# Swapping the two half-width sum buffers by block, scaling transposed tiles in pairs, and an off-diagonal product in three float32r products

## The chip, the core and the metric

The kernel runs on one core of a Trainium2 chip. Its parts are TensorE (PE in the profile, with its weight loads as PEld), VectorE (DVE), ScalarE (ACT), GpSimd (POOL) and SyncE (SP). SP and POOL issue most transfers. The time is the device time of one launch in microseconds; the kernel before has a median of 1587.96 us over 3 runs (1587.68 to 1588.22).

## The reference

A batch of one, 256 tokens of width 2048, goes through two layers, each with an RMS norm before and a residual after it, and a last RMS norm. Layer 1 is a Mamba-2 mixer with 64 heads of 64 in 8 groups; layer 2 is a forgetting attention with 32 heads of 128.

```python
proj = h @ w_in                                  # z | x,B,C | dt
xbc = silu(causal_depthwise_conv(xbc, conv_w, conv_b))
dt = softplus(dt_raw + dt_bias); a = -exp(a_log)
xdt = xs * dt; acs = cumsum(dt * a)
y = (C B^T * exp(acs_l - acs_s), causal) @ xdt + xs * d_skip
y = gated_group_rmsnorm(y, z, norm_w) @ w_out    # layer 1
q, k, v, z, f = split(h @ w_in)                  # layer 2
logits = q k^T / sqrt(128) + cum_l - cum_s       # cum = cumsum(log_sigmoid(f + b))
y = (softmax(logits, causal) @ v * silu(z)) @ w_out
```

Everything is float32. The reference forms the Mamba mixer in chunks of 64 tokens; the result is that of the one causal sum above.

## The kernel before

**Products.** A large product is made from float32r parts: `act_hi` (ACT) writes the rounded part of an operand, `dve_lo` (DVE) the remainder, and three products, high by high, high by low and low by high, add up in one PSUM bank. Weights come through `prep` (line 153 issues the load on SP) or, for sums of weight blocks, through `prep_sum` (lines 170 to 207). `run` walks a list of parts, each some 2.7 us of PE work or half of that; the weights of a part are loaded, summed and split three parts ahead (`AHEAD`). `later(n, f)` asks for `f` after n parts, and only the PE instructions that it issues are queued behind the part's products.

**Who sets the order.** The program is handed to a planner. It puts every instruction of an engine into one fixed order, by the time at which its inputs and its buffer are planned to be ready, ties by the order of the program. At run time each engine and each queue (SP's and POOL's among them) works strictly through that order.

**Mamba, groups 0 to 7** (`group_units`). A group is made of column tiles: B, C, four tiles of x (two heads each) and 512 columns of z. A tile of x goes through the convolution and SiLU as `xT` (columns on the partitions), then `xa_pe` turns its two blocks of 128 tokens and `xa_dve` scales what stands in PSUM three times: by dt (`xd`), by the decay to the end of the first block (`xg`, first block only), by D (`xa`). `cb_dve` makes `cb`, three 128x128 blocks of C B^T with mask: first by first block of tokens, first by second, second by second. `decay` turns `acsB` (cumulated decays, spread over partitions by a POOL transfer, tag of two buffers) into `ee`; `y_pe` makes the two diagonal blocks (`py`, line 707), `off_pe` the one off the diagonal (`pof`, line 712), one float32 product of 128x128 by 128x512, and `off_dve` scales it by the decay and adds it to `xa`. Then follow `gate`, `norm` (line 755) and the turn for the output product (`out_pe`, `pyt`). Groups 2 to 7 run pair by pair between the parts of the output product of the pair before (`sum_units`).

**Attention, eight rounds of four heads** (`four_heads`). A round has two blocks of 1024 output columns, qk and vz (`block_units`). The first ten k-tiles of a block are multiplied through seven sums of weight blocks, of which three chains are kept, named a, b and c, with two k-tiles per sum; in rounds 1 to 7 a third sum has one k-tile, and is half as wide (512). In the order of a block, `STEPS`, chain a runs from the first step (A0, into `psx`) to the last (A2, into `psy`), chain c is the second step (C0, into `psv`), chain b runs from B0 to B1, the last step but one. The half-width sums of a and b don't lie in the seven `raw` buffers but in `forms`: tags `gh` and `gl` have six buffers each, the forms of x hold five of each through all rounds, and one of each is left. Before the change, a always takes `gh` and b always `gl`:

```python
elif wide < 1024 and name != "c":
    t = gp.tile([P, 7, P], F32, tag="gh" if name == "a" else "gl",
                name=f"sum_{name}").rearrange("p m s -> p (m s)")
```

In the trace, `sum_a<-in_wf_h` and `sum_b<-in_wf_h` on SP are the first loads of the half-width sums; `in_wf_s` belongs to the wide ones. Line 186 issues them. Line 200 adds b to a (step A3), line 193 adds b to `term` (step B1), after which b's buffer is free; a's is free after its last split for A2. Between vz and the next qk of rounds 1 to 5 lies an output product (`out_f`, `psa`, some 22 us); between qk and vz of a round lies nothing.

Of the kernel before, what the change touches and what calls it, by code (L numbers as in the profile page):

```python
# [17 lines left out]
P = 128  # L18
# [51 lines left out]
def hybrid_kernel(ctx: ExitStack, tc: tile.TileContext, a):  # L70
# [33 lines left out]
    def act_hi(out, in_, scale=None):  # L104
        if scale is None:
            nc.scalar.activation(out, in_, AF.Copy)  # L106
        else:
            nc.scalar.activation(out, in_, AF.Copy, scale=scale)  # L108
# [16 lines left out]
    def later(n, fn):  # L125

        events.setdefault(now[0] + 2 * n, []).append(fn)
# [44 lines left out]
    def prep_sum(u):  # L172


        name, src, how = u["chain"]
        wide = u.get("wide", 1024)
        if how == "load":
            if u.get("apart"):
                t = fp[0].tile([P, 1024], F32, tag="sum", name=f"sum_{name}")
            elif wide < 1024 and name != "c":  # L180
                t = gp.tile([P, 7, P], F32, tag="gh" if name == "a" else "gl",
                            name=f"sum_{name}").rearrange("p m s -> p (m s)")
            else:
                t = wp.tile([P, 1024], F32, tag="raw", name=f"sum_{name}", bufs=RAW)
            u["sums"][name] = t[:, :wide]
            nc.sync.dma_start(u["sums"][name], src)
            if wide < 1024 and name == "c":
                u["sums"]["t"] = t = fp[0].tile([P, wide], F32, tag="term", name="term")
                nc.sync.dma_start(t, u["term"])
        elif how == "add" and "term" in u:  # L190
            t = u["sums"]["t"]
            if name == "b":
                nc.vector.tensor_tensor(t, t, u["sums"]["b"], op=ALU.add)
                u["sums"]["b"] = t
            else:
                nc.vector.tensor_tensor(u["sums"][name], u["sums"][name], t, op=ALU.add)
        elif how == "add":
            behind["POOL"] = nc.gpsimd.dma_start(u["sums"][name], src, accum_op=ALU.add).ins  # L198
        else:
            nc.vector.tensor_tensor(u["sums"][name], u["sums"][name], u["sums"][how], op=ALU.add)  # L200
        raw = u["sums"][name]
        wh = wp.tile([P, 1024], F32R, tag="wh", name="wh")[:, :wide]
        wl = wp.tile([P, 1024], F32R, tag="wl", name="wl", bufs=4)[:, :wide]
        act_hi(wh, raw)
        behind["DVE"] = dve_lo(wl, raw, wh).ins
        u["w"][0] = (wh, wl)
        yield
# [379 lines left out]
    def group_units(g):  # L587
# [2 lines left out]
        wait = 5 if g == 0 else 0  # L590
        more = 4 if g == 0 else 0

        def heads_of(tab, i, n):

            ap = tab[:, H0 + 2 * i:H0 + 2 * i + 2].unsqueeze(2).to_broadcast([P, 2, HD])
            return ap.unsqueeze(1).to_broadcast([P, n, 2, HD]) if n > 1 else ap

        def post_b(ps):
            conv_silu(ps, 6 * g, f"BT{g}", lambda o: st.update(B=o))
# [15 lines left out]
        def cb_dve():  # L615
            st["cb"] = cb = lp.tile([P, 384], F32, tag="cb", name=f"cb{g}", bufs=2)
            nc.vector.tensor_tensor(cb, st["pcb"][:, :384], cst[:, C_MQ:C_MQ + 384],
                                    op=ALU.mult)

        def post_x(i):  # L620
            def post(ps):
                conv_silu(ps, 6 * g + 2 + i, f"xT{g}_{i}", lambda o: x_done(i, o))
                later(2 + wait, lambda: load_acs(i))
            return post
# [7 lines left out]
        def x_done(i, o):  # L632
            st[f"x{i}"] = o
            if g == 0:
                later(1 + wait, lambda: xa_pe(i))
                later(2 + wait, lambda: xa_dve(i))
            elif i % 2:
                st["first"], st["then"] = ((cb_pe,), (cb_dve, lambda: st["mul0"]())) if i == 1 else (
                    (lambda: y_pe(0), lambda: y_pe(1)), ())
                later(2, lambda: [f() for f in (lambda: xa_pe(i - 1), lambda: xa_pe(i),  # L640
                                                *st["first"])])
                later(3, lambda: [f() for f in (*st["then"], lambda: xa_dve(i - 1),
                                                lambda: xa_dve(i))])
            later(2 + wait + more, lambda: decay(i))
            if g == 0:
                later(4 + wait + more, lambda: y_pe(i))
            if i == 3:
                if g > 0:
                    later(5, lambda: [y_pe(2), y_pe(3)])
                late = wait + more or 1  # L650
                later(4 + late, off_pe)
                later(5 + late, off_dve)

        def xa_pe(i):
            st[f"pxa{i}"] = pt = bank(psa, "pxa")
            for t in range(T2):
                nc.tensor.transpose(pt[:, t * P:t * P + P], st[f"x{i}"][:, t * P:t * P + P],
                                    ident)

        def xa_dve(i):  # L660
            if i == 0:
                xa = lp.tile([P, 4 * (S + 1)], F32, tag="xa", name=f"xa{g}", bufs=2)
                st["xa"] = xa[:, :T2 * 512].rearrange("p (t c) -> p t c", t=T2)
                xd = lp.tile([P, 4 * (S + 1)], F32, tag="xd", name=f"xd{g}")
                st["xd"] = xd[:, :T2 * 512].rearrange("p (t c) -> p t c", t=T2)
                st["xg"] = lp.tile([P, 512], F32, tag="xg", name=f"xg{g}")
            c = slice(i * P, i * P + P)
            pt = st[f"pxa{i}"]
            pt4 = pt[:, :S].rearrange("p (t h d) -> p t h d", t=T2, h=2)
            d = dts[:, :, H0 + 2 * i:H0 + 2 * i + 2].unsqueeze(3).to_broadcast([P, T2, 2, HD])  # L670
            nc.vector.tensor_tensor(
                st["xd"][:, :, c].rearrange("p t (h d) -> p t h d", h=2), pt4, d, op=ALU.mult)
            nc.vector.tensor_tensor(
                st["xg"][:, c].rearrange("p (h d) -> p h d", h=2), pt4[:, 0],
                heads_of(gdt, i, 1), op=ALU.mult)
            nc.vector.tensor_tensor(
                st["xa"][:, :, c].rearrange("p t (h d) -> p t h d", h=2), pt4,
                heads_of(row[:, R_D:R_D + MH], i, T2), op=ALU.mult)

        def decay(i):  # L680
            ee = lp.tile([P, 2, T2, P], F32, tag="ee", name="ee", bufs=3)
# [17 lines left out]
        def y_pe(i):  # L699
# [3 lines left out]
            for j in range(2):  # L703
                hl = 2 * i + j
                c = slice(hl * HD, hl * HD + HD)
                for t in range(T2):
                    nc.tensor.matmul(st["py"][t][:, c], m[:, j, t, :], st["xd"][:, t, c],  # L707
                                     start=True, stop=True)

        def off_pe():  # L710
            st["pof"] = bank(psa, "pof")
            nc.tensor.matmul(st["pof"], st["cb"][:, P:2 * P], st["xg"], start=True, stop=True)

        def off_dve():
            yo = sp.tile([P, 512], F32, tag="zth", name="yo")
# [291 lines left out]
    def block_units(w_s, w_p, out, scale, done, order):  # L1007
# [71 lines left out]
        for step in order[0]:  # L1079
            if step == "enter":  # L1080
                entering = len(parts)
                continue
            if step in (0, 1):
                parts.append(order[1][step])
                continue
            if step in n_rest:
                n = n_rest[step]
                n_rest[step] += 1
                names = ("v", "y") if step == "L" else ("z", "u")
                u = us[step]  # L1090
                parts.append({"u": u, "h": [n],
                              "mm": lambda u=u, n=n, names=names: mm_rest(u, n, names)})
                if n + 1 == len(u["w"]) and step == "L":
                    parts[-1]["post"] = left if order[0] is not SECOND else (
                        lambda: [left(), later(1, late_form)])
                continue
            chain, term, how, form, name = step
            for p2 in range(len(pairs)):
                u = {"chain": (chain, w_s[p2][term], how), "sums": sums[p2], "w": [None],
                     "wide": 512 * pairs[p2],  # L1100
                     "apart": chain == "b" and p2 == 0 and order[0] is not FIRST}
                if pairs[p2] == 1 and (chain == "c" or term == 1):
                    u["term"] = w_s[p2][1]
                steps[0] += pairs[p2] == 1
                parts.append({"u": u, "h": [0], "long": 1 if pairs[p2] == 2 else steps[0] % 2,
                              "mm": lambda u=u, form=form, name=name, p2=p2:
                                  mm_sum(u, form, name, p2)})
            if (chain, term) in reads:
                parts[-1]["post"] = reads[chain, term]
                if (chain, term) == ("b", 1) and n_rest["R"] == len(us["R"]["w"]):  # L1110
                    parts[-1]["post"] = lambda: [reads["b", 1](), right()]
# [8 lines left out]
    def four_heads(hq, first=()):  # L1120
# [139 lines left out]
        def weights(n):  # L1260
# [3 lines left out]
            if hq == 0:  # L1264
# [1 line left out]
            return [s1[0], s1[1], s2], rest  # L1266

        return [block_units(*weights(n), out, scale, done,
                            (FIRST, first) if hq == n == 0 else (SECOND if hq == 0 else STEPS, ()))
                for n, (out, scale, done) in enumerate((  # L1270
                    (lambda: bp.tile([P, T2, 1024], F32, tag=f"x{hq % 2}", name=f"qk{hq}"),
                     lambda: lay2["rstQ"], qk_done),
# [174 lines left out]
```

## Time and profile before

| | |
|---|---|
| median of 3 runs | 1587.96 us (1587.68 to 1588.22) |
| the profiled execution | 1588.28 us, its span 1586.5 us |
| granted TensorE clock, mean | 0.999 |
| busy: PE, DVE, ACT, POOL | 1570.5, 1374.1, 1078.5, 178.1 us |
| the share of the span in the chain that ended last: PE, issue, DVE, DMA, ACT | 91, 3, 2, 2, 1% |
| `sum_a<-in_wf_h` on that chain | 1.2% |
| Mamba groups, output products between them | about 5 to 640 us |
| attention rounds and their output products | about 640 us to the end |

A row of the timeline gives the start, the duration, engine, line, operation, output and inputs, how many like instructions stand in the row, and in brackets the idle time before it and what ended it. Matmuls overlap: one of 512 columns is shown as some 390 ns long, while the next starts some 227 ns after it. So what PE loses is read from the starts, not from its busy time.

### The profile page before, as it was taken

The numbers are of one execution on the slowest core, as the hardware profiler recorded it, in microseconds if no ns is written. First come the engines' busy times: TensorE is split into PE (matmuls) and PEld (weight loads), VectorE is DVE, ScalarE is ACT, GpSimd is POOL, SyncE is SP. The second block draws the span as 40 slices with busy tenths as digits, with TensorE's granted clock in tenths as the row PEclk, the third lists the DMA queues.
The fourth block names the chain that finished last, engine by engine and source line by source line (L and its number), as shares of the span: only waits on it lengthen the run. The fifth ranks groups of instructions, "written<-read, shape, count | busy, mean of one in ns | idle before, by whom it ended". The sixth has DMA issues, their size and how long they took to land.

```text
span 1586.5 us, 22866 instructions
## 1 busy us (share of the span) xinstructions
PE 1570.5 (99%) x7760; PEld 1318.8 (83%) x7760; DVE 1374.1 (87%) x2087; ACT 1078.5 (68%) x1694; POOL 178.1 (11%) x225
## 2 busy tenths in 40 slices
PE   9999999999999999999999999999999999999997
PEld 7888888888888888878888888888888888888886
DVE  7897989798979898799888898889888888889886
ACT  7677676767676765766776675766676666777764
POOL 0000111011100110011101110110110111011100
PEclk9999999999999999999999999999999999999999
DMA  9665798769886987579888788798886996899852
GB/s 367 192 215 186 189 276 224 257 177 275 222 265 175 270 226 232 186 170 267 247 246 281 192 231 266 223 227 264 215 259 206 252 276 165 245 270 251 249 178 80
DMA packets 106406, 364.54 MB, mean 230 GB/s; under 512 B 12176, under 2 KB 13072, under 8 KB 106160
## 3 DMA queue, kind: packets, MB, share of 16 engines
q1 hardware_dynamic: 79344, 270.03, 48.6%
q0 software_dynamic: 26800, 92.91, 30.5%
q8 instruction: 61, 1.00, 0.3%
q14 instruction: 57, 0.47, 0.1%
q10 hardware_dynamic: 144, 0.13, 0.0%
HBM read 360.83 MB, written 2.20 MB: 229 GB/s over the span
## 4 chain that ended last, share of the span: by engine, by line
PE 91%; issue 3%; DVE 2%; DMA 2%; ACT 1%; POOL 0%; ACTq 0%; POOLq 0%; DVEq 0%
PE psa L132 22%; PE pst L132 15%; PE psx L132 13%; PE psz L132 10%; PE psv L132 8%; PE psu L132 8%; PE psy L132 7%; PE py L707 2%; DMA sum_a<-in_wf_h 1%; DVE wl L112 1%; PE pqk L1166 1%; PE psc L1184 1%; PE ppt L1216 1%; PE psc L1182 0%; PE po L1242 0%
## 5 line engine op out<-in xcount | busy, mean ns | idle before, releaser
L112 DVE TENSOR_TENSOR wl<-raw,wh 128x1024 fp32r<-128x1024 f32 (+2 forms) x343 | 411.9, 1211 | 52.2 <-issue 22.9
L106 ACT ACTIVATE wh<-raw 128x1024 fp32r<-128x1024 f32 (+2 forms) x343 | 356.1, 1051 | 133.6 <-PE psa L132 54.2
L106 ACT ACTIVATE wh<-sum_a 128x1024 fp32r<-128x1024 f32 (+1 forms) x232 | 220.2, 954 | 157.0 <-PE psu L132 35.6
L112 DVE TENSOR_TENSOR wl<-sum_a,wh 128x1024 fp32r<-128x1024 f32 (+1 forms) x232 | 250.5, 1092 | 23.2 <-ACT wh L106 16.1
L132 PE MATMUL pst<-x,wh 128*128 128x512 f32 (+1 forms) x800 | 204.6, 396 | 0.8 <-DVE wh L161 0.8
L132 PEld LDWEIGHTS pst<-x,wh 128*128 128x128 f32 (+1 forms) x800 | 145.8, 189 | 30.3 <-ACT x L108 1.5
L132 PE MATMUL psa<-wh,x 128*128 128x512 f32 x512 | 129.4, 392 | 0.0
L106 ACT ACTIVATE wh<-sum_b 128x1024 fp32r<-128x1024 f32 (+1 forms) x102 | 100.0, 1004 | 28.2 <-PE psa L132 12.0
L112 DVE TENSOR_TENSOR wl<-sum_b,wh 128x1024 fp32r<-128x1024 f32 (+1 forms) x102 | 115.4, 1146 | 3.8 <-ACT wh L106 2.4
L132 PEld LDWEIGHTS pst<-x,wl 128*128 128x128 f32 x768 | 106.5, 191 | 8.8 <-DVE wl L112 0.3
L132 PEld LDWEIGHTS psa<-wh,x 128*128 128x128 f32 x512 | 95.5, 188 | 20.0 <-issue 0.5
L132 PE MATMUL pst<-x,wl 128*128 128x256 f32 x768 | 109.3, 283 | 0.0
L198 POOL DMA_DIRECT2D sum_a<-in_wf_s x64 | 55.3, 865 | 406.5 <-DMA raw<-in_wf_p 119.9
L132 PE MATMUL psz<-wh,x 128*128 128x512 f32 x200 | 78.7, 393 | 0.0
L132 PE MATMUL psv<-wh,x 128*128 128x512 f32 x200 | 78.2, 391 | 0.0
L132 PE MATMUL psu<-wh,x 128*128 128x512 f32 x200 | 78.0, 390 | 0.0
L132 PE MATMUL psy<-wh,x 128*128 128x512 f32 x200 | 78.0, 390 | 0.0
L132 PE MATMUL psx<-wh,ghx 128*128 128x512 f32 x234 | 77.8, 399 | 0.0
L132 PE MATMUL psx<-wl,ghx 128*128 128x512 f32 x234 | 76.3, 393 | 0.0
L132 PE MATMUL psx<-wh,glx 128*128 128x512 f32 x234 | 76.0, 391 | 0.0
L800 DVE TENSOR_TENSOR xs<-psa,xs 128x512 f32<-128x512 f32 (+1 forms) x81 | 51.9, 679 | 22.6 <-PE psa L132 22.2
L132 PE MATMUL psa<-wh,ghf 128*128 128x512 f32 (+1 forms) x260 | 71.1, 392 | 0.0
(359 smaller groups left out, 3365.3 us busy)
## 6 DMA issues: line engine op xcount, KB each, us to landing
raw<-in_wf_p SPq DMA_DIRECT2D x96, 512.0 KB, 4.7
raw<-in_wm_t SPq DMA_DIRECT2D x90, 512.0 KB, 5.1
raw<-in_wm_z SPq DMA_DIRECT2D x64, 512.0 KB, 5.7
sum_a<-in_wf_s POOLq DMA_DIRECT2D x64, 512.0 KB, 8.5
raw<-in_wf_o SPq DMA_DIRECT2D x64, 512.0 KB, 6.4
sum_a<-in_wm_s POOLq DMA_DIRECT2D x36, 512.0 KB, 6.8
sum_a<-in_wf_s SPq DMA_DIRECT2D x32, 512.0 KB, 6.9
sum_c<-in_wf_s SPq DMA_DIRECT2D x32, 512.0 KB, 9.3
```

The lines of the kernel that those rows point to most:

```text
L106: nc.scalar.activation(out, in_, AF.Copy)
L112: return nc.vector.tensor_tensor(out, in_, hi.bitcast(F32), op=ALU.subtract)
L132: behind["PE"] = nc.tensor.matmul(*args, **kw).ins
L198: behind["POOL"] = nc.gpsimd.dma_start(u["sums"][name], src, accum_op=ALU.add).ins
L707: nc.tensor.matmul(st["py"][t][:, c], m[:, j, t, :], st["xd"][:, t, c], start=True, stop=True)
L800: nc.vector.tensor_tensor(c, pss[t][:, a:b], c, op=ALU.add)
L1166: nc.tensor.transpose(pt[:, n * P:n * P + P], st["qk"][:, t, c:c + FD], ident)
L1184: nc.tensor.matmul(ps[:, P:P + S], q[:, :P], k[:, P:], start=j == 0, stop=j == 2)
L1216: nc.tensor.transpose(pt[:, c:c + P], uu[:, c:c + P], ident)
```

## The change

Three edits. The half-width sums of a and b change places in the second block of a round: a takes `gh` in qk and `gl` in vz, b the other one each time (`order` of `block_units` gets a third entry, true for the block qk). In groups 1 to 7, two tiles of x are turned into one PSUM bank, and each of the three scalings runs over both at once; group 0 stays as it was. In all groups the off-diagonal product is made from float32r parts: the middle block of `cb` is split right after it is made (tile `cbo`, one buffer), `xg` is split in a new step `off_split` one part ahead of `off_pe`, into two tiles under the tag `acsB`, and three products take the place of one.

```diff
@@ -178,7 +178,7 @@
             if u.get("apart"):
                 t = fp[0].tile([P, 1024], F32, tag="sum", name=f"sum_{name}")
             elif wide < 1024 and name != "c":
-                t = gp.tile([P, 7, P], F32, tag="gh" if name == "a" else "gl",
+                t = gp.tile([P, 7, P], F32, tag="gh" if (name == "a") == u["even"] else "gl",
                             name=f"sum_{name}").rearrange("p m s -> p (m s)")
             else:
                 t = wp.tile([P, 1024], F32, tag="raw", name=f"sum_{name}", bufs=RAW)
@@ -590,10 +590,11 @@
         wait = 5 if g == 0 else 0
         more = 4 if g == 0 else 0
 
-        def heads_of(tab, i, n):
-
-            ap = tab[:, H0 + 2 * i:H0 + 2 * i + 2].unsqueeze(2).to_broadcast([P, 2, HD])
-            return ap.unsqueeze(1).to_broadcast([P, n, 2, HD]) if n > 1 else ap
+        def heads_of(tab, i, m, n):
+
+            m *= 2
+            ap = tab[:, H0 + 2 * i:H0 + 2 * i + m].unsqueeze(2).to_broadcast([P, m, HD])
+            return ap.unsqueeze(1).to_broadcast([P, n, m, HD]) if n > 1 else ap
 
         def post_b(ps):
             conv_silu(ps, 6 * g, f"BT{g}", lambda o: st.update(B=o))
@@ -616,6 +617,10 @@
             st["cb"] = cb = lp.tile([P, 384], F32, tag="cb", name=f"cb{g}", bufs=2)
             nc.vector.tensor_tensor(cb, st["pcb"][:, :384], cst[:, C_MQ:C_MQ + 384],
                                     op=ALU.mult)
+
+            st["cbo"] = c2 = lp.tile([P, 2, P], F32R, tag="cbo", name="cbo", bufs=1)
+            act_hi(c2[:, 0], cb[:, P:2 * P])
+            dve_lo(c2[:, 1], cb[:, P:2 * P], c2[:, 0])
 
         def post_x(i):
             def post(ps):
@@ -637,10 +642,9 @@
             elif i % 2:
                 st["first"], st["then"] = ((cb_pe,), (cb_dve, lambda: st["mul0"]())) if i == 1 else (
                     (lambda: y_pe(0), lambda: y_pe(1)), ())
-                later(2, lambda: [f() for f in (lambda: xa_pe(i - 1), lambda: xa_pe(i),
+                later(2, lambda: [f() for f in (lambda: xa_pe(i - 1, 2),
                                                 *st["first"])])
-                later(3, lambda: [f() for f in (*st["then"], lambda: xa_dve(i - 1),
-                                                lambda: xa_dve(i))])
+                later(3, lambda: [f() for f in (*st["then"], lambda: xa_dve(i - 1, 2))])
             later(2 + wait + more, lambda: decay(i))
             if g == 0:
                 later(4 + wait + more, lambda: y_pe(i))
@@ -648,34 +652,38 @@
                 if g > 0:
                     later(5, lambda: [y_pe(2), y_pe(3)])
                 late = wait + more or 1
+                later(3 + late, off_split)
                 later(4 + late, off_pe)
                 later(5 + late, off_dve)
 
-        def xa_pe(i):
+        def xa_pe(i, n=1):
+
             st[f"pxa{i}"] = pt = bank(psa, "pxa")
-            for t in range(T2):
-                nc.tensor.transpose(pt[:, t * P:t * P + P], st[f"x{i}"][:, t * P:t * P + P],
-                                    ident)
-
-        def xa_dve(i):
+            for j in range(n):
+                for t in range(T2):
+                    c = (t * n + j) * P
+                    nc.tensor.transpose(pt[:, c:c + P], st[f"x{i + j}"][:, t * P:t * P + P],
+                                        ident)
+
+        def xa_dve(i, n=1):
             if i == 0:
                 xa = lp.tile([P, 4 * (S + 1)], F32, tag="xa", name=f"xa{g}", bufs=2)
                 st["xa"] = xa[:, :T2 * 512].rearrange("p (t c) -> p t c", t=T2)
                 xd = lp.tile([P, 4 * (S + 1)], F32, tag="xd", name=f"xd{g}")
                 st["xd"] = xd[:, :T2 * 512].rearrange("p (t c) -> p t c", t=T2)
                 st["xg"] = lp.tile([P, 512], F32, tag="xg", name=f"xg{g}")
-            c = slice(i * P, i * P + P)
+            c, m = slice(i * P, i * P + n * P), 2 * n
             pt = st[f"pxa{i}"]
-            pt4 = pt[:, :S].rearrange("p (t h d) -> p t h d", t=T2, h=2)
-            d = dts[:, :, H0 + 2 * i:H0 + 2 * i + 2].unsqueeze(3).to_broadcast([P, T2, 2, HD])
+            pt4 = pt[:, :n * S].rearrange("p (t h d) -> p t h d", t=T2, h=m)
+            d = dts[:, :, H0 + 2 * i:H0 + 2 * i + m].unsqueeze(3).to_broadcast([P, T2, m, HD])
             nc.vector.tensor_tensor(
-                st["xd"][:, :, c].rearrange("p t (h d) -> p t h d", h=2), pt4, d, op=ALU.mult)
+                st["xd"][:, :, c].rearrange("p t (h d) -> p t h d", h=m), pt4, d, op=ALU.mult)
             nc.vector.tensor_tensor(
-                st["xg"][:, c].rearrange("p (h d) -> p h d", h=2), pt4[:, 0],
-                heads_of(gdt, i, 1), op=ALU.mult)
+                st["xg"][:, c].rearrange("p (h d) -> p h d", h=m), pt4[:, 0],
+                heads_of(gdt, i, n, 1), op=ALU.mult)
             nc.vector.tensor_tensor(
-                st["xa"][:, :, c].rearrange("p t (h d) -> p t h d", h=2), pt4,
-                heads_of(row[:, R_D:R_D + MH], i, T2), op=ALU.mult)
+                st["xa"][:, :, c].rearrange("p t (h d) -> p t h d", h=m), pt4,
+                heads_of(row[:, R_D:R_D + MH], i, n, T2), op=ALU.mult)
 
         def decay(i):
             ee = lp.tile([P, 2, T2, P], F32, tag="ee", name="ee", bufs=3)
@@ -707,9 +715,17 @@
                     nc.tensor.matmul(st["py"][t][:, c], m[:, j, t, :], st["xd"][:, t, c],
                                      start=True, stop=True)
 
+        def off_split():
+            st["off"] = xs2 = [lp.tile([P, 512], F32R, tag="acsB", name=f"xg{i}", bufs=2)
+                               for i in "hl"]
+            act_hi(xs2[0], st["xg"])
+            dve_lo(xs2[1], st["xg"], xs2[0])
+
         def off_pe():
             st["pof"] = bank(psa, "pof")
-            nc.tensor.matmul(st["pof"], st["cb"][:, P:2 * P], st["xg"], start=True, stop=True)
+            for n, (i, j) in enumerate(((0, 0), (0, 1), (1, 0))):
+                nc.tensor.matmul(st["pof"], st["cbo"][:, i], st["off"][j],
+                                 start=n == 0, stop=n == 2)
 
         def off_dve():
             yo = sp.tile([P, 512], F32, tag="zth", name="yo")
@@ -1097,7 +1113,7 @@
             chain, term, how, form, name = step
             for p2 in range(len(pairs)):
                 u = {"chain": (chain, w_s[p2][term], how), "sums": sums[p2], "w": [None],
-                     "wide": 512 * pairs[p2],
+                     "wide": 512 * pairs[p2], "even": order[2],
                      "apart": chain == "b" and p2 == 0 and order[0] is not FIRST}
                 if pairs[p2] == 1 and (chain == "c" or term == 1):
                     u["term"] = w_s[p2][1]
@@ -1266,7 +1282,7 @@
             return [s1[0], s1[1], s2], rest
 
         return [block_units(*weights(n), out, scale, done,
-                            (FIRST, first) if hq == n == 0 else (SECOND if hq == 0 else STEPS, ()))
+                            (FIRST if hq == n == 0 else SECOND if hq == 0 else STEPS, first, n == 0))
                 for n, (out, scale, done) in enumerate((
                     (lambda: bp.tile([P, T2, 1024], F32, tag=f"x{hq % 2}", name=f"qk{hq}"),
                      lambda: lay2["rstQ"], qk_done),
```

## The prediction

> **What bounds the kernel now.** I read the page, then the windows by stage, then PE's own waits. A measurement of this kernel can tell about 0.2%, 3.2 us, from no change; every difference below is held against that.
>
> ```profile
> span 1586.5 us, 22866 instructions
> ...
> 160.00:640.00 480.00, 480.00 (x2498) 409.82 (x2497) 427.94 (x670) 326.60 (x490) 56.82 (x73) 1.00 0.82 231
> 740.00:1480.00 740.00, 736.83 (x3492) 613.51 (x3491) 647.06 (x890) 505.08 (x778) 95.11 (x112) 1.00 0.85 238
> ...
> PE psv L132 <- DVE wl L112: 3.2, 7, 0.6
> ```
>
> The columns of the windows are the stretch, its length, then busy PE, PEld, DVE, ACT and POOL. PE is busy for all of the 480 us in which Mamba groups 2 to 7 run, and for 736.8 of 740 us in attention. Its clock is full (1.00). So only two things move the end: less PE work, or fewer PE stalls, and attention has one kind of stall: seven times a product of C0 into `psv` waits for its low split on DVE. What DVE or ACT gains elsewhere is worth nothing by itself.
>
> **One of the stalls in detail** (round 2, qk to vz), in the timeline:
>
> ```profile
> 900.03 0.33 SPq L186 DMA_DIRECT2D sum_b<-in_wf_h  x1
> ...
> 918.48 0.33 SPq L186 DMA_DIRECT2D sum_a<-in_wf_h  x1
> ...
> 923.48 0.63 ACT L106 ACTIVATE wh<-sum_a 128x512 fp32r<-128x512 f32 x1 [3.65 <-DMA sum_a<-in_wf_h]
> ...
> 924.15 0.69 DVE L112 TENSOR_TENSOR wl<-sum_a,wh 128x512 fp32r<-128x512 f32 x1 [1.60 <-ACT wh L106]
> ...
> 925.49 2.96 DVE L112 TENSOR_TENSOR wl<-sum_c,wh 128x1024 fp32r<-128x1024 f32 x3
> ...
> 924.53 0.39 PE L132 MATMUL psx<-wh,glx 128*128 128x512 f32 x1
> 924.89 0.50 PE L132 MATMUL psx<-wl,ghx 128*128 128x512 f32 x1
> 925.24 0.62 PE L132 MATMUL psv<-wh,ghx 128*128 128x512 f32 x2
> 925.69 0.61 PE L132 MATMUL psv<-wh,glx 128*128 128x512 f32 x2
> 926.76 0.73 PE L132 MATMUL psv<-wl,ghx 128*128 128x512 f32 x2 [0.46 <-DVE wl L112]
> 927.33 0.49 PE L1216 MATMUL ppt<-cst,dd 128*128 128x128 f32 x3
> ```
>
> The half-width sum a of vz can only be loaded at 918.48, when `gh` is free of the a of qk, and it is there 4.9 us later. ACT stands 3.65 us, DVE 1.60 us, and the splits of sum c, which stand behind on both in-order engines, come late in their turn. What it costs is in the starts: four products between 925.24 and 926.76 would take 0.91 us at 0.227 each (two starts of 925.24 lie 0.45 before 925.69). From 924.53 to 926.76 six starts take 2.23 us in place of 1.36, and the next two 0.57 in place of 0.45: 0.87 + 0.12 = 0.99 us.
>
> The same load stands on the chain of waits in rounds 3, 4 and 6, and in the queue of round 5:
>
> ```profile
> 1030.32 4.90 DMA sum_a<-in_wf_h
> ...
> 1142.17 4.97 DMA sum_a<-in_wf_h
> ...
> 1365.77 4.93 DMA sum_a<-in_wf_h
> ...
> 1254.09 0.33 SPq L186 DMA_DIRECT2D sum_a<-in_wf_h  x1
> ```
>
> So five of the seven waits are of this kind. Round 1 is the control that the profile holds by chance: there the load is early, ACT stands behind PE and not behind the load, and the same products run at their pace (five starts from 813.86 to 815.00, 1.14 us):
>
> ```profile
> 810.63 0.63 ACT L106 ACTIVATE wh<-sum_a 128x512 fp32r<-128x512 f32 x1 [2.43 <-PE psy L132]
> ...
> 813.86 0.39 PE L132 MATMUL psx<-wl,ghx 128*128 128x512 f32 x1
> ...
> 815.00 0.62 PE L132 MATMUL psv<-wl,ghx 128*128 128x512 f32 x2
> ```
>
> The other two waits are the change of round without an output product between (rounds 0 to 1, 6 to 7):
>
> ```profile
> 761.73 0.61 ACT L106 ACTIVATE wh<-sum_a 128x512 fp32r<-128x512 f32 x1
> ...
> 771.09 0.73 PE L132 MATMUL psv<-wl,ghx 128*128 128x512 f32 x2 [0.57 <-DVE wl L112]
> ...
> 1421.04 0.50 PE L132 MATMUL psv<-wl,ghx 128*128 128x512 f32 x1 [0.39 <-DVE wl L112]
> ```
>
> In the first, the half sum was split 9 us ahead; DVE's order is at fault, and the swap does not touch it. I count nothing for either (bound: at most 0.57 + 0.39 plus a slow restart each, 1.4 us in all).
>
> **The swap.** In vz, a now takes `gl`, which is free where b of qk was done with: the trace already shows a load entering that buffer at 900.03, 18.45 us before 918.48. The load lands by about 905, where the split is asked for near 920. SP gains no instruction; two loads trade places, and the one that now stands earlier is as ready there as b's was. Late next is b of vz: it now enters `gh` at about 918.5 in place of 900. It is wanted by the last third of B0, behind C0, one L and two thirds of B0, or 15 + 12 + 12 products after 925.24: near 925.2 + 39 x 0.227 = 934.1, and its split starts three parts, some 5 us, ahead. With the 4.9 us of landing it is there at 923.4, 5 us early. So the five stalls go: 5 x 0.99 = **5.0 us**. Bounds: nothing gained, if sum c's splits are late without a's help; 5.0 + 1.4 = 6.4 if all seven go.
>
> **The off-diagonal product.**
>
> ```profile
> 616.12 1.08 PE L712 MATMUL pof<-xg,cb 128*128 128x512 f32 x2
> 616.63 1.03 PE L132 MATMUL psx<-wh,ghm 128*128 128x512 f32 x2
> 617.50 0.62 PE L132 MATMUL psx<-wh,glm 128*128 128x512 f32 x2
> ```
>
> One float32 product (two records) and two float32r ones take 617.50 - 616.12 = 1.38 us; without the two, 0.93. Three float32r products take 0.68. PE has no idle time to hide it in, so 0.25 x 8 groups = **2.0 us** are gained. Bounds: none, if the change of operand type costs at the end as it does now (0.93 covers such a restart), to 2.0. The Trainium skill (TensorE: Matmul & The Clock Gate, "Wait — 56ns, not 53.3ns?") gives 215.7 ns from start to start at 512 columns; this trace has 227. By the page alone three products would take 0.65, the gain here would be 2.3 us, and the sum below 0.3 us lower.
>
> The splits add per group, on ACT and on DVE, one instruction of 128x512 (0.63 and 0.69, as at 923.48 and 924.15) and one of 128x128, bounded by the same: at most 1.3 and 1.4 us, hidden while PE doesn't wait for them. `off_pe` now waits for ACT and then DVE after `xg`; behind it on PE waits everything. The narrowest group, and a full split on ACT:
>
> ```profile
> L106 ACT ACTIVATE wh<-raw 128x1024 fp32r<-128x1024 f32 (+2 forms) x343 | 356.1, 1051 | 133.6 <-PE psa L132 54.2
> ...
> 196.10 0.28 DVE L673 TENSOR_TENSOR xg<-pxa,gdt 128x128 f32<-128x128 f32 x1
> 196.30 0.42 DVE L676 TENSOR_TENSOR xa<-pxa,row 128x256 f32<-128x256 f32 x1
> 196.63 0.68 DVE L691 TENSOR_TENSOR ee<-ee,cb 128x512 f32<-128x512 f32 x1
> 197.23 1.22 DVE L112 TENSOR_TENSOR wl<-sum_b,wh 128x1024 fp32r<-128x1024 f32 x1
> ...
> 203.00 1.08 PE L712 MATMUL pof<-xg,cb 128*128 128x512 f32 x2
> ```
>
> From 196.38 to 203.00 there are 6.6 us. The pair of splits takes 1.3, and each full split that stands in front takes about 1.05 on ACT and 1.22 on DVE: one before each makes 3.6 us. Value 0; it begins to cost beyond 6.6.
>
> **The tag `acsB`.** Its two buffers now go to the two halves of `xg` before the next group's decays. I take it that a tag's buffers are handed out in the order of the program; the rows for it, of group 1:
>
> ```profile
> 135.59 1.08 PE L712 MATMUL pof<-xg,cb 128*128 128x512 f32 x2
> ...
> 143.13 1.29 DVE L729 SCALAR_TENSOR_TENSOR zs<-zth,psa 128x512 f32<-128x512 f32 x2 [2.41 <-ACT zth L728]
> 144.34 0.68 DVE L716 TENSOR_TENSOR yo<-pof,fdec 128x512 f32<-128x512 f32 x1
> ```
>
> `yo` shares a tag with `zth`, its input is ready by 136.7, DVE idles 2.41 us, and it still comes after the `zth` that the program names first. So POOL's loads for the next group's first two heads move from before `pof` to behind it, here past the 203.7 at which `pof` ends, and the ACT decays with them; on POOL's own queue they move past loads that add up sums, which can only go earlier for it. The next group multiplies by them a whole group later. Value 0; the bound is a PE that waits at `py`: up to one load and one decay per group, and PE has no such wait now (480 of 480 us).
>
> **Pairs of x tiles.** PE's turns are the same. DVE:
>
> ```profile
> L671 DVE TENSOR_TENSOR xd<-pxa,dts x32: 414/417/425, 67.7 to 606.6; 128x256 f32<-128x256 f32 x32
> L673 DVE TENSOR_TENSOR xg<-pxa,gdt x32: 278/284/294, 68.0 to 606.9; 128x128 f32<-128x128 f32 x32
> ...
> L716 DVE TENSOR_TENSOR yo<-pof,fdec x8: 684/692/694, 96.7 to 617.2; 128x512 f32<-128x512 f32 x8
> ```
>
> Two tiles cost 2 x (417 + 284 + 417) = 2236 ns; as one, about 692 + 417 + 692 = 1801. 14 pairs save 6.1 us of DVE, against at most 8 x 1.4 = 11 that the splits add. PE waits for neither: value 0. If that cover were gone, the difference of at most 5 us would be PE's; if PE had waited for DVE here, up to 6 would be won, but the 480 of 480 us exclude that.
>
> **The sum.** 5.0 + 2.0 = 7.0 us. The profiled execution took 1588.28 (span 1586.5 and 1.8 around it), 0.3 above the median of the runs; 1588.28 - 7.0 = 1581.3, against the median **1581.0 us**.
>
> **The rivals.**
> - *The next wait takes over (20%).* Without the load, the splits of c are still late by DVE's own order, as at 771.09. For it: DVE runs three in a row from 925.49 without idling. Against it: it idled 1.60 just before, more than the 0.99 lost, and round 1. If each of the five gives only a quarter, 1.2 + 2.0 = 3.2: 1584.8.
> - *All seven go (8%).* The planner's order around 1421.04 and 771.09 changes too: 1588.0 - 2.0 - 6.4 = 1579.6.
> - *The off product waits, and the kernel is slower (6%).* With four full splits before each half, the pair ends 4 x 1.05 + 0.63 + 4 x 1.22 + 0.69 = 10.4 us after `xg`. Where 6.6 us are to be had PE stands 3.8 us, and if all eight groups are so narrow, 30 us: 1588 - 7 + 30 = 1611. It decides from 6.6 us on, and outweighs the gain from 7.5 us on (0.9 x 8). Against it: the rows above show three shorter instructions and one full split behind `xg`.
> - *The swap doesn't free a earlier (6%)*, if the planner still puts its load where it was, behind a buffer asked for earlier: only the 2.0 are gained, 1586.0.
>
> **How the numbers follow.** The forecast holds 60%, with its own range 1579.5 to 1583.2 (a planner's order that shifts by a product or two in each round). The first rival's half above 1584.8, the last rival and a little of small losses at PE make "within 0.2%" 0.20; slower 0.06; the rest, 0.74, is faster. For 8 in 10 the range reaches from 1579.2 to 1586.0.
>
> **What would show it.** Swap: `sum_a<-in_wf_h` of vz issued some 18 us earlier and off the chain of waits, ACT's waits for it gone, `psv` waiting for `wl` twice, not seven times. Off product: three records some 0.23 apart per group, in 0.68 us, with no PE idle time before the first. Pairs: three rows of 14 per scaling with 692 and 417 ns. It is wrong if PE gets a wait at `pof`, at `py` or `pyt`, if `psz` waits for the split of b, or if `psv` goes on waiting in rounds 2 to 6.

## The result, and the profile after

Over six runs of each, the changed kernel takes 1601.66 us (1597.42 to 1603.24) against 1588.09 (1585.72 to 1589.93): a ratio of 1.0083, interval 1.0069 to 1.0097. Ratios here and below are of runs at the full granted clock (one of the kernel before, 1733.46 us at 0.85, and one of the sixth experiment, 2894.22 us at 0.779, stand outside) and need not be the quotient of the medians. It is slower by 13.6 us, where 7 us of gain were forecast. Its profiled execution took 1603.24 us. The page, and the same two stretches of the windows as before (Mamba groups 2 to 7, attention), read:

```profile
span 1601.5 us, 22853 instructions
```

```profile
160.00:640.00 480.00, 467.41 (x2426) 397.90 (x2425) 415.71 (x626) 318.44 (x489) 56.61 (x73) 0.99 0.81 224
740.00:1480.00 740.00, 739.77 (x3507) 618.18 (x3506) 652.15 (x897) 510.84 (x776) 96.58 (x114) 1.00 0.86 241
```

Attention did what was forecast: PE idles 0.2 us there in place of 3.2. Mamba did not: PE, which had not idled for 480 us, now idles 12.6, and its records in that stretch fall from 2498 to 2426. Two marks of the trace split the difference. The last Mamba group's first `pyt` starts at 641.53 before and at 662.23 after, 20.7 us later; from there to the end it is 945.0 us before and 939.3 after, 5.7 us less. 20.7 - 5.7 = 15.0, the difference of the spans.

PE's waits name who ends the stops (us in all, times, longest):

```profile
PE psx L132 <- DVE xs L849: 10.5, 6, 2.5
PE pyt L778 <- ACT xa L771: 2.1, 2, 1.8
...
PE psv L132 <- DVE wl L112: 0.2, 1, 0.2
```

Of the places in Mamba that the prediction watched (`pof`, `py`, `pyt`) only `pyt` is among them, and the largest wait, an output product that waits until DVE has added up the sum before it (`xs`, line 849), was not on its list. The waits of all engines show what else grew, ahead of DVE; of after, and then of before:

```profile
POOL acsB L633 <- PE pof L727: 66.1, 6, 23.4
...
ACT ee L693 <- DMA acsB<-acs_d: 39.9, 16, 6.1
```

```profile
POOL acsB L628 <- ACT ee L685: 112.1, 28, 16.4
...
ACT ee L685 <- DMA acsB<-acs_d: 13.4, 7, 3.6
```

The first load of `acsB` for a group waits for the `pof` of the group before, as forecast; ACT's wait for those loads has tripled. The timeline of after, where group 2 ends and group 3's decays are due, ties the two ends together (start, length, engine, in brackets the idle time before it and its end):

```profile
205.54 0.48 PE L727 MATMUL pof<-xgh,cbo 128*128 128x512 f32 x1
...
206.55 1.12 POOL L633 DMA_DIRECT2D acsB<-acs_d  x2 [1.96 <-PE pof L727]
207.45 1.06 ACT L106 ACTIVATE wh<-raw 128x1024 fp32r<-128x1024 f32 x1 [3.27 <-PE psz L132]
...
213.57 0.99 ACT L693 ACTIVATE ee<-acsB,beta 128x128 f32<-128x128 f32 x3 [5.06 <-DMA acsB<-acs_d]
...
214.46 1.04 ACT L106 ACTIVATE wh<-sum_b 128x1024 fp32r<-128x1024 f32 x1
...
215.54 1.22 DVE L112 TENSOR_TENSOR wl<-sum_b,wh 128x1024 fp32r<-128x1024 f32 x1 [3.61 <-ACT wh L106]
...
219.56 0.70 PE L132 MATMUL psx<-wh,ghm 128*128 128x512 f32 x2 [0.80 <-DVE xs L849]
...
229.82 0.68 DVE L849 TENSOR_TENSOR xs<-xs,psx 128x512 f32<-128x512 f32 x1
...
230.65 0.85 PE L132 MATMUL psx<-wh,ghm 128*128 128x512 f32 x2 [2.54 <-DVE xs L849]
```

Read from top to bottom it is a suspicion: the loads are issued behind `pof`, land 7 us later, ACT stands 5.06 us at the first of group 3's decays, the split of `sum_b` stands behind it, DVE stands 3.61 us for that split, and the additions behind it keep `psx` from PE. Before, at the same change, the first two loads were out before `pof` (193.88 and 196.52, `pof` at 203.00), and the first split of `sum_b` ran 6.85 us earlier, of which 2.54 is that this stage as a whole came earlier (`pof` at 203.00, not 205.54):

```profile
203.12 1.57 ACT L685 ACTIVATE ee<-acsB,beta 128x128 f32<-128x128 f32 x5 [1.51 <-DMA acsB<-acs_d]
...
207.61 1.04 ACT L106 ACTIVATE wh<-sum_b 128x1024 fp32r<-128x1024 f32 x1
```

The experiments ask whether it is the lent tag that does it, and through which of the two queues, POOL's or ACT's.

### The profile page after: what moved, and what is told of

It reads as the page before. It is cut to its first block, busy times and chain, and to the rows that moved or that the text cites. A ratio compares the mean times of both kernels' runs of the same rounds, so it can differ in the third digit from the quotient of the medians.

```text
span 1601.5 us, 22853 instructions
## 1 busy us (share of the span) xinstructions
PE 1574.5 (98%) x7768; PEld 1324.0 (83%) x7768; DVE 1377.4 (86%) x2061; ACT 1083.2 (68%) x1710; POOL 177.4 (11%) x225
## 4 chain that ended last, share of the span: by engine, by line
PE 86%; DVE 5%; issue 4%; DMA 2%; ACT 2%; POOL 0%; POOLq 0%; ACTq 0%; DVEq 0%
PE psa L132 21%; PE psx L132 13%; PE pst L132 11%; PE psz L132 9%; PE psv L132 8%; PE psu L132 8%; PE psy L132 8%; DMA acsB<-acs_d 2%; DVE wl L112 2%; PE py L715 2%; ACT wh L106 1%; PE pqk L1182 1%; PE psc L1200 1%; PE ppt L1232 1%; ACT ee L693 1%
## 5 line engine op out<-in xcount | busy, mean ns | idle before, releaser
L132 PE MATMUL pst<-x,wh 128*128 128x512 f32 (+1 forms) x800 | 207.9, 401 | 0.7 <-DVE wh L161 0.7
L112 DVE TENSOR_TENSOR wl<-sum_b,wh 128x1024 fp32r<-128x1024 f32 (+1 forms) x102 | 115.1, 1146 | 16.2 <-ACT wh L106 15.1
L106 ACT ACTIVATE wh<-sum_c 128x1024 fp32r<-128x1024 f32 (+1 forms) x58 | 54.5, 952 | 28.9 <-PE psa L132 17.4
L693 ACT ACTIVATE ee<-acsB,beta 128x128 f32<-128x128 f32 x128 | 42.3, 391 | 46.5 <-DMA acsB<-acs_d 39.9
```

Source lines behind the costliest of these rows:

```text
L112: return nc.vector.tensor_tensor(out, in_, hi.bitcast(F32), op=ALU.subtract)
L132: behind["PE"] = nc.tensor.matmul(*args, **kw).ins
L693: nc.scalar.activation(ee[:, j, t, :], st["acs"][i][:, j, t * P:t * P + P], AF.Relu, scale=-1.0, bias=beta[:, t, h:h + 1])
```

## The experiments

My theory was the chain above. Its rivals were that the two added splits, or the wait of PE for them, cost the time; that the paired tiles do; and that it is POOL's standing 66 us behind `pof`, with its sum loads behind that, and not ACT's.

**The whole change, with the halves of `xg` under another tag.** `zth` belongs to the group's own `yo` and gate, which come after `pof` anyway.

```diff
-            st["off"] = xs2 = [lp.tile([P, 512], F32R, tag="acsB", name=f"xg{i}", bufs=2)
+            st["off"] = xs2 = [sp.tile([P, 512], F32R, tag="zth", name=f"xg{i}")
```

> The whole change, but the two halves of xg lie under the tag zth, so that acsB keeps its two buffers for the decays. Nothing is left out. Theory (the lent acsB buffers cost everything: the loads of the next group's decays move behind pof, ACT's queue stands at their first relu, and the splits behind it come late): the Mamba part falls back from 662 us (last pyt) to about 640, the gains of attention (5.7 us) and of the product (2 us) stay, 1580 to 1583. Rival (the four extra splits per group, or the product's own wait for them, cost it): 1595 or more.

It took 1581.04 us (1579.63 to 1581.89), 0.9958 of before (0.9945 to 0.9971). So one tag turns 13.6 us of loss into 6.7 of gain (by the ratios). The waits of all engines, the windows and ACT's timeline at the same place:

```profile
POOL acsB L633 <- ACT ee L693: 126.8, 30, 15.4
...
ACT ee L693 <- DMA acsB<-acs_d: 12.2, 7, 2.7
```

```profile
160.00:640.00 480.00, 480.00 (x2509) 411.55 (x2508) 429.96 (x643) 330.36 (x502) 56.85 (x73) 1.00 0.82 232
```

```profile
202.14 1.28 ACT L693 ACTIVATE ee<-acsB,beta 128x128 f32<-128x128 f32 x4 [1.88 <-DMA acsB<-acs_d]
...
207.51 1.04 ACT L106 ACTIVATE wh<-sum_b 128x1024 fp32r<-128x1024 f32 x1
```

No load waits for `pof`, ACT's wait for them is what it was before the change, the split of `sum_b` is back at 207.51, and PE doesn't idle. All the splits and pairs are still there, so neither they nor PE's wait for them is the cause.

**The swap alone**, on the kernel before:

```diff
-                t = gp.tile([P, 7, P], F32, tag="gh" if name == "a" else "gl",
+                t = gp.tile([P, 7, P], F32, tag="gh" if (name == "a") == u["even"] else "gl",
```

> The kernel before with the swap of gh and gl alone. Theory: attention's 820.9 us from the first pqk to the end become 815.2, as in the changed kernel, and nothing else moves: 1582 to 1583. Rival (attention is faster because it now starts in another phase of the queues, which the Mamba part set): within 2 us of the kernel before.

1583.57 us, 0.9973 of before (0.9962 to 0.9984): 4.3 us faster, a little short of the 1582 to 1583 expected and clear of the rival's 2 us. The queue of loads and PE's line in round 2:

```profile
899.40 0.33 SPq L186 DMA_DIRECT2D sum_a<-in_wf_h  x1
...
917.85 0.33 SPq L186 DMA_DIRECT2D sum_b<-in_wf_h  x1
...
924.12 0.39 PE L132 MATMUL psx<-wl,ghx 128*128 128x512 f32 x1
...
924.80 0.62 PE L132 MATMUL psv<-wh,glx 128*128 128x512 f32 x2
...
925.26 0.62 PE L132 MATMUL psv<-wl,ghx 128*128 128x512 f32 x2
```

```profile
740.00:1480.00 740.00, 740.00 (x3520) 619.31 (x3519) 652.17 (x902) 513.15 (x790) 98.46 (x116) 1.00 0.85 239
```

The two loads have traded places (899.40 and 917.85), the products run at their pace, and PE does not idle at all in 740 us: all seven waits are gone, not the five.

**The three products alone, with the tag as in the change**, x tile by tile, no swap:

```diff
+            st["off"] = xs2 = [lp.tile([P, 512], F32R, tag="acsB", name=f"xg{i}", bufs=2)
...
-            nc.tensor.matmul(st["pof"], st["cb"][:, P:2 * P], st["xg"], start=True, stop=True)
+            for n, (i, j) in enumerate(((0, 0), (0, 1), (1, 0))):
+                nc.tensor.matmul(st["pof"], st["cbo"][:, i], st["off"][j],
+                                 start=n == 0, stop=n == 2)
```

> The kernel before with the off-diagonal product in three float32r products alone, halves of xg under acsB, x's scalings tile by tile. Theory (lent buffers): the Mamba part loses its 20.7 us here too, 1605 to 1611. Rival (the pairs of x tiles make the loss, by xT and cu that come late): 1585 to 1590.

1601.65 us, 1.0081 of before (1.0058 to 1.0104), less than the 1605 to 1611 expected and far from the rival. The loss is here, without pairs and without the swap, by the same waits:

```profile
POOL acsB L632 <- PE pof L724: 64.9, 6, 25.3
...
ACT ee L690 <- DMA acsB<-acs_d: 30.5, 15, 4.5
```

```profile
PE psx L132 <- DVE xs L846: 6.8, 4, 2.5
```

**The whole change, the tag left lent, but the decays put further back on ACT.** Each decay's ACT instructions are ordered behind the newest weight split:

```diff
-                act_hi(wh[:, c], raw[:, c])
+                behind["ACT"] = act_hi(wh[:, c], raw[:, c]).ins
...
-        act_hi(wh, raw)
+        behind["ACT"] = act_hi(wh, raw).ins
...
+            with tc.issue_after(behind["ACT"]):
+                for j in range(2):
...
+                nc.scalar.activation(ee, ee, AF.Exp, scale=-1.0)
```

> The whole change, acsB lent as in it, but decay's relus and exponential on ACT are queued behind the last split of weights that the program names before them. Theory (what costs is that ACT's in-order queue stands at a relu whose transfer is under way, not that the decays are late): the waits of psx for xs go, 1580 to 1588. Rival (the decays themselves are late, or POOL's queue is what holds the sums): PE waits at py or psx as before, 1598 or more.

1581.64 us, 0.9961 of before (0.9947 to 0.9975). This is the run that tells POOL's queue from ACT's:

```profile
POOL acsB L632 <- PE pof L727: 67.2, 6, 24.6
...
ACT ee L693 <- PE py L715: 6.6, 6, 1.1
```

```profile
205.92 1.06 ACT L106 ACTIVATE wh<-sum_b 128x1024 fp32r<-128x1024 f32 x1 [1.23 <-DVE wl L111]
...
247.79 0.39 ACT L693 ACTIVATE ee<-acsB,beta 128x128 f32<-128x128 f32 x1
```

The loads wait for `pof` as long as in the changed kernel (67.2 us against 66.1), and POOL stands as long, yet the time is that of the first experiment. Only ACT's wait for them is gone: the first decay of the next group runs at 247.79, 45 us after its load was issued (202.74). So the late load costs nothing, and POOL's standing costs nothing; ACT standing in front of the splits costs it all.

**The pairs alone**: `xa_pe` and `xa_dve` with two tiles in groups 1 to 7, on the kernel before.

> The kernel before with x's transposes scaled in pairs alone. Theory (DVE time that no product waits for is worth nothing): within 1.5 us of 1588, the Mamba part (last pyt) at 641.5 within 1 us. Rival (the pair, which waits for the later tile's turns, makes xT and cu late and costs 1 to 3 us in groups 2 to 7): 1590 to 1592.

1586.94 us against 1587.11, ratio 0.9998 (0.9989 to 1.0007), the last `pyt` at 640.99: nothing, though DVE's three scalings do shrink as worked out (the rows of `xd` in the changed kernel: 14 pairs and the 4 tiles of group 0):

```profile
L679 DVE TENSOR_TENSOR xd<-pxa,dts x18: 417/682/692, 67.1 to 627.1; 128x512 f32<-128x512 f32 x14, 128x256 f32<-128x256 f32 x4
```

**The three products alone under `zth`**, the third experiment with the tag of the first:

```diff
-            st["off"] = xs2 = [lp.tile([P, 512], F32R, tag="acsB", name=f"xg{i}", bufs=2)
+            st["off"] = xs2 = [sp.tile([P, 512], F32R, tag="zth", name=f"xg{i}")
```

> The kernel before with the three float32r products alone, the halves of xg under zth. Theory: PE does 8 times 0.24 us less and waits for nothing new: 1586 to 1587. Rival (the splits' place on ACT and DVE takes the gain back): 1588 or more.

1587.45 us against 1587.11, ratio 0.9998 (0.9989 to 1.0007), between the two expectations. This and the third experiment differ in the tag alone: 1.0081 against 0.9998, some 13 us. By itself, the off product in three parts gains nothing that can be measured. Why, the timeline shows:

```profile
615.73 0.48 PE L724 MATMUL pof<-xgh,cbo 128*128 128x512 f32 x1
616.04 0.39 PE L724 MATMUL pof<-xgl,cbo 128*128 128x512 f32 x1
616.27 0.39 PE L724 MATMUL pof<-xgh,cbo 128*128 128x512 f32 x1
616.50 0.63 PE L132 MATMUL psx<-wh,ghm 128*128 128x512 f32 x2
```

From the first start to the next product it is 0.77 us, where the prediction had 0.68 and the float32 product 0.93: the first, which follows the float32 `py`, takes 0.31 to the next start, the others 0.23.

**The swap and the three products under `zth`, x tile by tile**: the first experiment without pairs.

> The swap and the three products with the halves under zth, without the pairs. Theory (the parts add up, and the pairs are worth nothing): the same as the run e1_off_zth_tag within 1 us, 1580 to 1582. Rival (the pairs' 6 us of DVE made room for the four splits): 1583 or more.

1581.43 us, 0.9962 of before (0.9950 to 0.9975), as the first experiment (0.9958): the pairs are worth nothing in company either, and the four splits cost nothing without them.

**Both cures at once**: halves under `zth` and decays behind the splits.

> The whole change with the halves under zth, and the decays on ACT queued behind the splits of weights. Both cures of the one illness: if there is only that illness, the second adds nothing, 1580 to 1582. If decays in ACT's order still cost something with the buffers given back, 1578 to 1580.

1580.67 us, 0.9958 of before (0.9946 to 0.9971). Where ACT no longer stands, holding the decays back adds nothing. Every version that has the swap and doesn't let ACT stand beats both kernels (1580.67 to 1583.57 us); of those with the whole change, the first is the shortest edit.

## Why the prediction was wrong

**The step that failed is "The tag `acsB`", with its "Value 0; the bound is a PE that waits at `py`".** Its mechanism was right as far as it went: a tag's buffers are handed out in the order of the program, and the loads went behind `pof`. It then asked who needs the decays, found that nobody does for a whole group, and priced the delay at nothing. That answer was right too: in the fourth experiment the first of them runs 45 us behind its load (247.79 against 202.74), and it costs nothing. What it left out is what stands behind a decay on ACT: the planner's order has it in front of the splits for the output product, ACT takes its instructions in order, and an input that lands only 7 us after the issue at 206.55 holds up work that has no part in it. The Trainium skill (Perfetto Trace Analysis, "Tensor Engine Instruction (MATMUL, LD_WEIGHTS)") says that ACT, DVE and GpSimd are strict FIFO; the 5.06 us of ACT at 213.57, with a split right behind, agree. The prediction asked just this of POOL's queue and of PE's, and not of ACT's.

Its price can be laid out in the trace of after: 12.6 us of PE idle time in groups 2 to 7; 1.5 more than before at the `pyt` of 154.69, just ahead (1.81 against 0.33); and some 1.6 us in each of three stretches in which PE runs at half pace behind a stop (below), 4.8. Each of the ten added stops hides some 0.16 us more, since a product is shown as 0.39 long where the next could start after 0.227: an estimate of 1.6. That is 20.5, against the 20.7 by which Mamba ends later, plus the 1.2 or so that the off product should have saved there. The 1.4 us left over I can't attribute. Nor is it shown why the lent tag costs Mamba more in the whole change (20.7) than in the third experiment, whose mark is at 656.66 (15.1): its trace has fewer stops (8.4 us in groups 2 to 7) and two stretches at half pace.

**The rival on the slower side** had the wrong place: no run's list of PE's waits names `pof`, so the splits of `xg` fit into the 6.6 us, as worked out. (The `pof` that the prediction lets end at 203.7 ends at 204.08 by its own row; nothing hangs on it.)

**The swap** was right in mechanism: loads at 899.40 and 917.85 where 900 and 918.5 were forecast, off the path, stalls of rounds 2 to 6 gone. Its size was about right too. In the changed kernel the four rounds from 880.05 to 1323.62 take 443.57 us against 447.29 before (859.70 to 1306.99), 0.93 each, the forecast's 0.99 nearly. The rest of the 5.7 us is the two waits at changes of round which I counted at nothing (bound 1.4); all but 0.2 us of them vanished, why is not shown, so the rival "all seven go" was the case. It isn't sure to be: in the first experiment one of them came back, larger (PE's waits list `psv` for `wl` once, 1.6 us), and attention gains 4.4, from 944.97 to 940.58. In the trace of the swap alone it gains 6.1 (to 938.83), while its runs gain 4.3 us by the ratio, with 2.5 to 6.0 as the interval: 5.0 can't be told from 6.4 by them.

**The off product** was priced at 0.25 a group; the trace has 0.15 to 0.16, 1.2 us in eight groups, too little to be seen in the sixth experiment. The term that was sized wrong is "0.68": it took three float32r products at their running pace and left out that the first follows `py` and takes 0.31. The bound below it, a cost at the change of type, pointed the right way.

**The pairs** were right at 0. The cover that they were to give the splits wasn't needed: without pairs the splits cost nothing that can be measured (sixth and seventh experiments), so the bound of 5 us was never tried.

That the first experiment lands on the forecast's 1581.0 is partly luck: between the marks the swap gave 4.4 for 5.0, the off product 1.2 for 2.0, and Mamba in that run ends 2.3 us earlier (639.22 against 641.53), of which only 1.2 has a cause in these rows.

## What to carry to other kernels

When a step delays an input, ask of each engine that reads it not only who needs the result, but what stands behind the reading instruction on that engine's queue: a prefetch that is early by a whole group still has to be there when its reader's turn comes. Buffers lent by a prefetch cost its lead; take them from a tag whose next user comes later anyway, or move the reader back. And a wait's releaser in PE's list (`xs` on DVE here) can be two engines away from the cause, so follow the idle times backwards until one ends at something that moved.

## What the runs showed of the hardware

Short stops of PE were followed by a low clock. In the timeline of after, the products behind the stop of 2.54 us at 230.65 come to start 0.43 us apart (231.29 to 232.14 for two) in place of 0.227; three more stops stand beside it:

```profile
154.69 0.33 PE L778 MATMUL pyt<-cst,xa 128*128 128x128 f32 x1 [1.81 <-ACT xa L771]
...
230.65 0.85 PE L132 MATMUL psx<-wh,ghm 128*128 128x512 f32 x2 [2.54 <-DVE xs L849]
231.29 1.06 PE L132 MATMUL psx<-wh,glm 128*128 128x512 f32 x2
232.14 1.06 PE L132 MATMUL psx<-wl,ghm 128*128 128x512 f32 x2
...
400.35 0.70 PE L132 MATMUL psx<-wh,ghm 128*128 128x512 f32 x2 [2.12 <-DVE xs L849]
...
570.28 0.70 PE L132 MATMUL psx<-wh,ghm 128*128 128x512 f32 x2 [2.07 <-DVE xs L849]
```

In the windows, PE's busy time stands behind the length, and the granted clock is the third number from the end. Three stretches, behind the first three stops, are at half; behind the stop at 570.28 the clock stays full:

```profile
152.54:155.95 3.41, 1.31 (x10) 0.92 (x10) 2.62 (x8) 3.29 (x8) 0.87 (x1) 1.00 0.48 157
155.95:159.36 3.41, 3.41 (x12) 2.74 (x10) 3.34 (x8) 2.84 (x6) 0.00 (x0) 0.50 0.53 171
231.05:234.45 3.40, 3.40 (x10) 2.65 (x9) 2.54 (x7) 2.33 (x5) 0.71 (x1) 0.50 0.75 264
401.71:405.12 3.41, 3.41 (x10) 2.63 (x9) 2.67 (x4) 2.29 (x3) 0.70 (x1) 0.50 0.77 255
565.55:568.96 3.41, 2.67 (x16) 2.19 (x14) 3.41 (x5) 2.92 (x5) 0.00 (x0) 1.00 0.36 117
568.96:572.37 3.41, 2.08 (x9) 1.79 (x10) 2.55 (x5) 2.35 (x5) 0.71 (x1) 1.00 0.70 239
```

The half clock lasts 3.41 us each time, and in that time 3.41 x (1 - 0.227 / 0.425) = 1.6 us of work are lost. The Trainium skill (TensorE: Matmul & The Clock Gate, "What's actually happening") puts the half clock behind an idle window of about 3.4 us; the stretches here have that length, but some 2 us of idle time in the one ahead were enough.

What decides can be read from the starts. They lie 75.1 and 170.7 us apart, which is 22 and 50 times 3.413, so the three fit one fixed grid. The 3.41 us ahead of each hold 2.10, 2.54 and 2.05 us of idle PE (the first is 3.41 - 1.31). On that grid the stop of 2.07 us at 570.28 is cut in two, 0.74 and 1.33 us, the last two rows. The third experiment has two such stretches, from 228.97 and 563.47 (98 times 3.413 apart), behind 2.51 and 2.39 us in one piece, and none behind its stop of 1.42 at 395.62. Cut into such pieces from end to end, both traces show the clock halved right behind each piece that held 2.05 us of idle time or more, and behind none that held 1.42 or less. That is an inference from a few stretches; no run moved a stop to try it.

The other thing is the start of `pof`: 0.31 us from a first float32r product behind the float32 `py` to the next start, against 0.23 from then on. Whether the change of operand type makes it, or that the products of `py` are short (64 columns), no run separates.
